# A decoder layer on one core: opening rewritten around the tokens, normalized tokens spread over the units that precede their use, stores from two queues

## The chip, the core and the metric

The kernel runs on one core of a Trainium2 chip. TensorE multiplies matrices (PE in the profile, its weight loads PEld), VectorE (DVE) and ScalarE (ACT) do elementwise work, and transfers between the main memory and the on-chip memory go through the core's 16 DMA engines; a transfer is started from the queue of SyncE (SP) or of ScalarE. The engines run side by side and wait for each other by semaphores, each working through its own list of instructions in order. The metric is the device time of one execution in microseconds; lower is better.

## The reference, cut to what matters

One decoder layer on 256 tokens of width 2048, in float32:

```
mod = silu(c) @ w_ada + b_ada                    # 2048 -> 6 x 2048: shift, scale, gate, twice
h   = rms_norm(x, norm1_g) * (1 + scale1) + shift1
lru_x, lru_gate, q, k, v, g_a, g_b = split(h @ w_in)
y_a = (rg_lru(conv4(lru_x)) * gelu(lru_gate)) @ w_lru_out
y_b = sliding_window_attention(q, k, v, sinks, bias) @ w_attn_out
x   = x + gate1 * ((sigmoid(g_a)*y_a + sigmoid(g_b)*y_b) @ w_out)
h2  = rms_norm(x, norm2_g) * (1 + scale2) + shift2
x   = x + gate2 * (relu(h2 @ w_ff1)**2 @ w_ff2)  # 2048 -> 8192 -> 2048
out = rms_norm(x, final_g)
```

## The kernel before, in words

*Layout.* Tokens lie along the free dimension: a tile is 128 channels by 256 tokens, and the width of 2048 is `KT` = 16 such tiles. A weight comes as units of 128 by 2048 float32 (1 MB), sixteen blocks of 128 by 128.

*Products.* A float32 product is made of three cheaper ones. Each operand is cut into a high part, rounded to the type `fp32r`, and the rest: `w_split` makes `wh` on ScalarE (L162) and `wl` on VectorE (L164) in two halves of 1024 columns, and `split` does the same for an activation tile (L143, L144). `gemm` then issues, for every block, `wh`·high, `wh`·low and `wl`·high into one PSUM tile (L178 to L180); `gemm_wide` joins the first two into one matmul of 512 columns (L191 to L194). Raw weights have four buffers (`RAW_BUFS`), `wh` and `wl` three each (`WH_BUFS`). All loads go through SyncE's queue in its order, so a load whose buffer is not free holds those behind it.

*Conditioning.* `mod` needs a product of one row with 96 units of weights. It is done on VectorE: `scr` holds silu(c) in every partition, and `ada_unit` loads a unit and reduces it against `scr` (L262, 128 by 2048). Two such units give shift and scale of one tile of `h`. 96 of them are scattered over the kernel by a credit.

*Opening.* Two small loads (`vc` with all vectors, `idt` the identity), eight loads of tokens of 128 by 512 (`xtok`, L97), all from SyncE. The line `scr` is built in four quarters by a multiply on VectorE (L222), a matmul with ones (L224) and a copy (L225). Squares of the tokens are summed, four on VectorE (L234) and four on ScalarE (L237); `rstd_cols` makes the factor per token in six small steps; VectorE scales the eight token pieces (L243); 32 transposes (L249) and eight copies (L251) turn them into channel-major tiles `xs`. Then two conditioning units give `a1` (L276), ScalarE applies shift and scale (L278), and `split` gives `h[j]`.

*Early passes.* So that TensorE need not wait for all sixteen `h`, the input projection first runs over `h[0:2]` for 56 output tiles (seven units), then `h[2:6]`, then `h[6:10]`, adding into `res` (L331 to L335); the rest of it comes in the main list of units.

*Main list.* Loads and splits are written two units ahead (`LOOK`); after a unit's `run`, side work is taken from a list by credit. The first nine units of the first feed-forward product (`run_first`, L687 to L689) start before the second normalization is known: they use un-normalized tiles `z` and multiply by the row factor in the eviction (L691 to L695). Units from the tenth on (`ZN_FROM` = 9) use normalized tiles `zn`, made by `make_zn` (L646, L647 and `split`), which come from the side list, all sixteen put there at the last output unit.

*End.* x is transposed back (L786), scaled by the last row factor, alternately on VectorE (L803) and ScalarE (L801), and written by eight stores from SyncE's queue (L804).

*Order.* A planner places the instructions on each engine, by its own model of durations and by the order in which they are written; it may put a later one first. `keep_in_program_order` pins an instruction behind the one that was written just before it on the same engine. Before, the pins that matter here are on reductions 0 and 4 only.

## Time and profile before

| what | value |
|---|---|
| three runs | 1597.89 us median (1596.14 to 1598.55) |
| the profiled execution | 1596.44 us, of which the span is 1594.7 us |
| TensorE / VectorE / ScalarE busy | 97% / 77% / 56% of the span |
| moved by DMA | 387.90 MB, 243 GB/s on average |

The span runs from the first to the last recorded instruction of one execution; the 1.7 us beside it lie outside it. "Busy" of TensorE is modelled from its pipelined matmuls. In a row of instructions the engine and the line of the kernel come first, then what is written and read with shapes, a count, and in brackets the idle time ahead and what ended it. A releaser is the one that came last.

### The profile page before, as it was taken

To read this page: it belongs to the slowest core of one execution; us is meant where nothing else is said; L and a number is where in the kernel's file an instruction comes from. 1 tells how busy PE (TensorE), PEld (TensorE's weight loads), DVE (VectorE), ACT (ScalarE), POOL (GpSimd) and SP (SyncE) were. 2 spreads that over 40 slices of the span, in tenths; PEclk is the share of its full clock that TensorE was granted. 3 is DMA by queue.
4 is the path that set the end of the run, shared out by engine and by line. 5 is a ranking of instruction groups with operands and counts; after the bars stand their busy time and mean duration, and the time that the engine had idled before them with its cause. 6 is when DMAs were issued, how large, how long until landed. Compare 5 with 4: busy or idle time off the path is not lost.

```text
span 1594.7 us, 24929 instructions
## 1 busy us (share of the span) xinstructions
PE 1552.5 (97%) x9804; PEld 1388.1 (87%) x9804; DVE 1220.7 (77%) x1947; ACT 888.5 (56%) x1508; POOL 0.2 (0%) x4
## 2 busy tenths in 40 slices
PE   4999999999999999999999999999999999999997
PEld 3999998899988888888888988888888888888886
DVE  6798998898989879788898867865565556655664
ACT  5733447687786564445456764356534664356554
POOL 0000000000000000000000000000000000000000
PEclk7999999999999999999999999999999999999999
DMA  8898985657768768778885667875555555555552
GB/s 315 330 341 318 340 287 196 214 180 243 277 234 301 264 230 304 284 290 294 320 314 207 221 243 271 320 266 185 185 186 187 189 192 194 189 185 185 185 187 78
DMA packets 61702, 387.90 MB, mean 243 GB/s; under 512 B 6576, under 2 KB 11024, under 8 KB 19216
## 3 DMA queue, kind: packets, MB, share of 16 engines
q1 hardware_dynamic: 57168, 381.95, 65.7%
q10 hardware_dynamic: 4416, 4.35, 1.0%
q8 instruction: 77, 1.26, 0.3%
q14 instruction: 41, 0.34, 0.1%
HBM read 384.13 MB, written 2.15 MB: 242 GB/s over the span
## 4 chain that ended last, share of the span: by engine, by line
PE 89%; DVE 5%; ACT 2%; issue 2%; DMA 1%; SPq 0%; ACTq 0%; DVEq 0%
PE pg L192 45%; PE pg L191 21%; PE pg L180 5%; PE pg L178 5%; PE pg L179 5%; DVE wl L164 2%; PE pg L207 2%; PE pg L194 1%; PE pg L689 1%; PE pg L687 1%; PE pg L688 1%; PE pa L491 1%; PE pa L498 1%; DVE ra L262 1%; ACT wh L162 1%
## 5 line engine op out<-in xcount | busy, mean ns | idle before, releaser
L192 PE MATMUL pg<-k,wh 128*128 128x512 f32 x3120 | 1080.4, 395 | 0.3 <-DVE k L144 0.3
L164 DVE TENSOR_TENSOR wl<-rw,wh 128x1024 fp32r<-128x1024 f32 (+2 forms) x534 | 628.3, 1178 | 281.8 <-ACT wh L162 275.2
L162 ACT ACTIVATE wh<-rw 128x1024 fp32r<-128x1024 f32 (+2 forms) x534 | 544.2, 1022 | 525.9 <-PE pg L192 365.3
L191 PE MATMUL pg<-k,wl 128*128 128x256 f32 x2925 | 819.9, 280 | 0.1
L192 PEld LDWEIGHTS pg<-k,wh 128*128 128x128 f32 x3120 | 573.6, 188 | 121.3 <-PE pg L192 0.6
L191 PEld LDWEIGHTS pg<-k,wl 128*128 128x128 f32 x2925 | 552.2, 189 | 9.5 <-DVE wl L164 0.4
L178 PE MATMUL pg<-k,wh 128*128 128x256 f32 x832 | 237.4, 287 | 10.4 <-ACT k L143 8.9
L180 PE MATMUL pg<-k,wl 128*128 128x256 f32 x832 | 233.9, 284 | 3.7 <-DVE wl L164 3.6
L179 PE MATMUL pg<-k,wh 128*128 128x256 f32 x832 | 235.0, 283 | 0.2 <-DVE k L144 0.2
L262 DVE CUSTOM_DVE_ANT_0 ra<-ra,scr,vc 128x2048 f32<-128x2048 f32 x96 | 225.1, 2346 | 9.7 <-DMA ra<-in_wada_dram 9.6
L178 PEld LDWEIGHTS pg<-k,wh 128*128 128x128 f32 x832 | 157.4, 190 | 12.9 <-ACT k L143 9.4
L180 PEld LDWEIGHTS pg<-k,wl 128*128 128x128 f32 x832 | 157.2, 190 | 6.0 <-DVE wl L164 4.7
L179 PEld LDWEIGHTS pg<-k,wh 128*128 128x128 f32 x832 | 157.9, 190 | 1.2 <-DVE k L144 0.5
L712 DVE SCALAR_TENSOR_TENSOR k<-pg,mod,k 128x256 f32<-128x256 f32 x128 | 61.9, 483 | 31.8 <-PE pg L192 29.5
L701 ACT ACTIVATE t<-t 128x256 f32<-128x256 f32 x55 | 22.9, 417 | 70.5 <-DVE t L199 70.5
L194 PE MATMUL pg<-k,wl 128*128 128x256 f32 x195 | 55.2, 283 | 2.1 <-DVE wl L164 2.1
L199 DVE TENSOR_TENSOR t<-pg,t 128x256 f32<-128x256 f32 x131 | 54.7, 418 | 0.0
L198 ACT ACTIVATE t<-pg 128x256 f32<-128x256 f32 x131 | 47.8, 365 | 1.7 <-PE pg L192 1.7
L194 PEld LDWEIGHTS pg<-k,wl 128*128 128x128 f32 x195 | 36.6, 188 | 10.7 <-DVE wl L164 2.8
L687 PE MATMUL pg<-z,wh 128*128 128x258 f32 x144 | 41.6, 289 | 2.0 <-ACT wh L162 2.0
L689 PE MATMUL pg<-z,wl 128*128 128x258 f32 x144 | 41.5, 289 | 0.9 <-DVE wl L164 0.9
L688 PE MATMUL pg<-z,wh 128*128 128x256 f32 x144 | 41.7, 290 | 0.0
(158 smaller groups left out, 959.1 us busy)
## 6 DMA issues: line engine op xcount, KB each, us to landing
rw<-in_w_f_dram SPq DMA_DIRECT2D x204, 1024.0 KB, 4.9
ra<-in_wada_dram SPq DMA_DIRECT2D x96, 1024.0 KB, 6.5
rw<-in_w_p_dram SPq DMA_DIRECT2D x31, 1024.0 KB, 6.7
rw<-in_w_r_dram SPq DMA_DIRECT2D x20, 768.0 KB, 4.9
rw<-in_w_r_dram SPq DMA_DIRECT2D x16, 640.0 KB, 4.0
bt<-ud ACTq DMA_DIRECT2D x8, 512.0 KB, 4.2
xt<-in_xt_dram SPq DMA_DIRECT2D x8, 256.0 KB, 6.5
lw<-in_lruw_dram SPq DMA_DIRECT2D x4, 512.0 KB, 5.8
```

The source lines that it names most:

```text
L162: se.activation(wh[:, :c], raw[:, o:o + c], AF.Copy)
L164: ve.tensor_tensor(out=wl[:, :c], in0=raw[:, o:o + c], in1=wh[:, :c].bitcast(F32), op=ALU.subtract)
L178: te.matmul(ps, lhsT=wh[:, w], rhs=hl[:, 0], start=k == 0, stop=False)
L179: te.matmul(ps, lhsT=wh[:, w], rhs=hl[:, 1], start=False, stop=False)
L180: te.matmul(ps, lhsT=wl[:, w], rhs=hl[:, 0], start=False, stop=k == n - 1)
L191: te.matmul(ps[:, 0], lhsT=wl[:, w], rhs=hl[:, 0], start=False, stop=False)
L192: te.matmul(ps, lhsT=wh[:, w], rhs=hl, start=k == 0, stop=k == n - 1)
L194: te.matmul(ps[:, 0], lhsT=wl[:, w], rhs=hl[:, 0], start=False, stop=False)
L262: r = ve.tensor_tensor_reduce(out=raw, in0=raw, in1=scr, scale=1.0, scalar=vc[:, V_BADA + c:V_BADA + c + 1], op0=ALU.mult, op1=ALU.add, ac ...
L687: te.matmul(ps, lhsT=wh[:, e], rhs=z[k][:, 0:258], start=k == 0, stop=False)
L688: te.matmul(ps[:, 0:256], lhsT=wh[:, e], rhs=z[k][:, 258:514], start=False, stop=False)
L712: ve.scalar_tensor_tensor(out=x1[f], in0=ps[:, i], scalar=mod[:, 5 * KT + f:5 * KT + f + 1], in1=x1[f], op0=ALU.mult, op1=ALU.add)
```

## The change

- *Loads.* `vc` and `idt` are started from ScalarE's queue. The tokens come as four loads of 128 by 1024 from SyncE, into buffers of `wh` and `wl` that no weights use yet (two of three each). The first four conditioning units (`ada_dma`) and the first weight unit (`first_raw`) are issued from fixed places.
- *Line.* `line_quarter` transposes a broadcast column of `sc` sixteen times in place of multiply and matmul with ones.
- *Squares.* Five on VectorE and three on ScalarE, interleaved with the line's copies in a written order.
- *Turning.* Per quarter (`turn_in`), VectorE scales one half of the tokens and ScalarE the other.
- *Order.* Nearly all VectorE and ScalarE work of the opening is pinned (`pin`): turn quarters 0 and 1, reductions 0 and 1, split the first half of the first weights, `h[0]`, reduction 2, the second half, reduction 3, turn quarter 2, `h[1]`, turn quarter 3. Reductions 4 to 11 are pinned too; reduction 4 was before.
- *Normalized tokens.* `make_zn` is no longer on the side list. Unit f of `run_first` makes tiles 2f and 2f+1 after its own eviction, and their first step is pinned.
- *Stores.* Odd pieces are stored from ScalarE's queue, even ones from SyncE's.

`split` loses an argument that nothing used.

```diff
...
 ADA_LAST, QUIET_OUT, QUIET_FF1 = 0.3, 2, 3
 LOOK, CREDIT, Z_FROM, ADA_RATE, ADA_FIRST = 2, 2.3, 12, 0.45, 0.85
 
-ZN_FROM, ZN_COST = 9, 1.0
+ZN_FROM = 9
 
 PASSES = [(0, 2, 56), (2, 6, 56), (6, 10, 40)]
 NATIVE = {(2, u) for u in range(0, 56, 16)}
...
         return pa.tile(list(shape), F32, tag="pa", name=nm("pa"))
 
 
+    pin = tc.keep_in_program_order
     vc = cp.tile([P, NV], F32, name="vc")
-    nc.sync.dma_start(out=vc, in_=vec)
+    pin(se.dma_start(out=vc, in_=vec))
     idt = cp.tile([P, P], F32, name="idt")
-    nc.sync.dma_start(out=idt, in_=ident)
+    pin(se.dma_start(out=idt, in_=ident))
+
     xtok = {}
-    for b in range(2):
-        for q in range(4):
-            xtok[b, q] = kp.tile([P, 512], F32, tag="k2", name=nm("xt"))
-            nc.sync.dma_start(out=xtok[b, q], in_=xt[b, :, q * 512:(q + 1) * 512])
+    for i in range(2):
+        for b, tag in ((0, "wh"), (1, "wl")):
+            xh = wp.tile([P, WCH], F32R, tag=tag, name=nm(tag), bufs=WH_BUFS).bitcast(F32)
+            pin(nc.sync.dma_start(out=xh, in_=xt[b, :, i * WCH:(i + 1) * WCH]))
+            for q in range(2):
+                xtok[b, 2 * i + q] = xh[:, q * 512:(q + 1) * 512]
     ones = cp.tile([P, P], F32, name="ones")
     ve.memset(ones, 1.0)
     eps = cp.tile([P, 1], F32, name="eps")
     ve.memset(eps, EPS)
 
...
-    def w_split(raw, n):
+    def w_split(raw, n, pin=lambda i: i, o0=0):
         parts = []
-        for o in range(0, n, WCH):
-            c = min(WCH, n - o)
+        for o in range(o0, o0 + n, WCH):
+            c = min(WCH, o0 + n - o)
             wh = wp.tile([P, WCH], F32R, tag="wh", name=nm("wh"), bufs=WH_BUFS)
-            se.activation(wh[:, :c], raw[:, o:o + c], AF.Copy)
+            pin(se.activation(wh[:, :c], raw[:, o:o + c], AF.Copy))
             wl = wp.tile([P, WCH], F32R, tag="wl", name=nm("wl"), bufs=WH_BUFS)
-            ve.tensor_tensor(out=wl[:, :c], in0=raw[:, o:o + c], in1=wh[:, :c].bitcast(F32), op=ALU.subtract)
+            pin(ve.tensor_tensor(out=wl[:, :c], in0=raw[:, o:o + c], in1=wh[:, :c].bitcast(F32), op=ALU.subtract))
             parts.append((wh, wl))
         return parts
 
...
 
 
     sc = cp.tile([P, KT], F32, name="sc")
-    tc.keep_in_program_order(se.activation(sc, vc[:, V_C:V_C + KT], AF.Sigmoid))
-    ve.tensor_tensor(out=sc, in0=sc, in1=vc[:, V_C:V_C + KT], op=ALU.mult)
-
-    tc.keep_in_program_order(se.activation(tmp([P, 1]), ones[:, 0:1], AF.Sqrt))
+    pin(se.activation(sc, vc[:, V_C:V_C + KT], AF.Sigmoid))
+    pin(ve.tensor_tensor(out=sc, in0=sc, in1=vc[:, V_C:V_C + KT], op=ALU.mult))
+
+    pin(se.activation(tmp([P, 1]), ones[:, 0:1], AF.Sqrt))
     scr = cp.tile([P, KT * P], F32, name="scr")
-    for q in range(4):
-        pc = bank([P, 512])
-        dg = tmp([P, 512])
-        ve.tensor_tensor(out=dg.rearrange("p (k f) -> p k f", k=4), in0=idt[:, None, :].broadcast_to((P, 4, P)),
-                         in1=sc[:, 4 * q:4 * q + 4, None].broadcast_to((P, 4, P)), op=ALU.mult)
-        te.matmul(pc, lhsT=ones, rhs=dg, start=True, stop=True)
-        se.activation(scr[:, q * 512:(q + 1) * 512], pc, AF.Copy)
-
-
     ssq = sp.tile([P, 2, 4], F32, tag="ssq", name="ssq", bufs=1)
     ss1 = sp.tile([P, 2], F32, tag="ss1", name="ss1", bufs=1)
-    for b in range(2):
-        for q in range(4):
-            xq = xtok[b, q]
-            if b == 0:
-                ve.tensor_tensor_reduce(out=tmp([P, 512]), in0=xq, in1=xq, scale=1.0, scalar=0.0, op0=ALU.mult,
-                                        op1=ALU.add, accum_out=ssq[:, b, q:q + 1])
-            else:
-                se.activation(tmp([P, 512]), xq, AF.Square, accum_out=ssq[:, b, q:q + 1])
-    ve.tensor_reduce(out=ss1, in_=ssq, axis=mybir.AxisListType.X, op=ALU.add)
-    rs1 = rstd_cols(ss1)
+    def line_quarter(q):
+        pc = bank([P, 512])
+        for i in range(4):
+
+            k = 4 * q + i
+            te.transpose(pc[:, i * P:(i + 1) * P], sc[:, k:k + 1].broadcast_to((P, P)), idt)
+        pin(se.activation(scr[:, q * 512:(q + 1) * 512], pc, AF.Copy))
+
+    def square_dve(b, q):
+        pin(ve.tensor_tensor_reduce(out=tmp([P, 512]), in0=xtok[b, q], in1=xtok[b, q], scale=1.0, scalar=0.0,
+                                    op0=ALU.mult, op1=ALU.add, accum_out=ssq[:, b, q:q + 1]))
+
+    def square_act(b, q):
+        pin(se.activation(tmp([P, 512]), xtok[b, q], AF.Square, accum_out=ssq[:, b, q:q + 1]))
+
+
+    line_quarter(0)
+    square_dve(0, 0)
+    square_dve(0, 1)
+    square_act(1, 0)
+    square_act(1, 1)
+    line_quarter(1)
+    line_quarter(2)
+    square_dve(0, 2)
+    square_dve(0, 3)
+    square_act(1, 2)
+    square_dve(1, 3)
+    line_quarter(3)
+    pin(ve.tensor_reduce(out=ss1, in_=ssq, axis=mybir.AxisListType.X, op=ALU.add))
+    rs1 = rstd_cols(ss1, pin)
     xs = []
-    for q in range(4):
-        for b in range(2):
-            ve.tensor_scalar(out=xtok[b, q], in0=xtok[b, q], scalar1=rs1[:, b:b + 1], scalar2=None, op0=ALU.mult)
+
+    def turn_in(q):
+
+        pin(ve.tensor_scalar(out=xtok[0, q], in0=xtok[0, q], scalar1=rs1[:, 0:1], scalar2=None, op0=ALU.mult))
+        pin(se.activation(xtok[1, q], xtok[1, q], AF.Copy, scale=rs1[:, 1:2]))
         for j in (2 * q, 2 * q + 1):
             px = bank([P, 512])
             for i in range(2):
...
                     e = (2 * (j % 2) + i) * P
                     te.transpose(px[:, i * T + b * P:i * T + (b + 1) * P], xtok[b, q][:, e:e + P], idt)
             xs.append(pair())
-            se.activation(xs[j].rearrange("p a b -> p (a b)"), px, AF.Copy)
+            pin(se.activation(xs[j].rearrange("p a b -> p (a b)"), px, AF.Copy))
+
 
     mod = cp.tile([P, 6 * KT], F32, name="mod")
     ada_next = [0]
-
-    def ada_unit():
+    same = lambda i: i
+
+    def ada_dma(pin=same):
+        raw = wp.tile([P, KT * P], F32, tag="raw", name=nm("ra"), bufs=RAW_BUFS)
+        pin(nc.sync.dma_start(out=raw, in_=wada[ada_next[0] + len(ada_raw)]))
+        ada_raw.append(raw)
+
+    ada_raw = []
+
+    def ada_unit(pin=same):
+        if not ada_raw:
+            ada_dma()
+        raw = ada_raw.pop(0)
         n = ada_next[0]
         ada_next[0] += 1
-        raw = wp.tile([P, KT * P], F32, tag="raw", name=nm("ra"), bufs=RAW_BUFS)
-        nc.sync.dma_start(out=raw, in_=wada[n])
         c = ADA_ORDER[n]
-        r = ve.tensor_tensor_reduce(out=raw, in0=raw, in1=scr, scale=1.0, scalar=vc[:, V_BADA + c:V_BADA + c + 1],
-                                    op0=ALU.mult, op1=ALU.add, accum_out=mod[:, c:c + 1])
-
-        if n in (0, 4):
-            tc.keep_in_program_order(r)
+
+        if 2 * PASSES[0][1] <= n < 2 * PASSES[0][1] + 8:
+            pin = tc.keep_in_program_order
+        pin(ve.tensor_tensor_reduce(out=raw, in0=raw, in1=scr, scale=1.0, scalar=vc[:, V_BADA + c:V_BADA + c + 1],
+                                    op0=ALU.mult, op1=ALU.add, accum_out=mod[:, c:c + 1]))
         return n
 
     h = [None] * KT
     a1 = cp.tile([P, KT], F32, name="a1")
+
     def ada_norm1():
         n = ada_unit()
         if n % 2 == 1:
-            j = n // 2
-            xj = xs[j // 2][:, j % 2]
-            ve.scalar_tensor_tensor(out=a1[:, j:j + 1], in0=mod[:, KT + j:KT + j + 1], scalar=1.0,
-                                    in1=vc[:, V_G1 + j:V_G1 + j + 1], op0=ALU.add, op1=ALU.mult)
-            se.activation(xj, xj, AF.Identity, scale=a1[:, j:j + 1], bias=mod[:, j:j + 1])
-            h[j] = split(xj)
-
-    for _ in range(2 * PASSES[0][1] - 2):
-        ada_norm1()
+            norm1_tile(n // 2)
+
+    def norm1_tile(j, pin=same):
+        xj = xs[j // 2][:, j % 2]
+        pin(ve.scalar_tensor_tensor(out=a1[:, j:j + 1], in0=mod[:, KT + j:KT + j + 1], scalar=1.0,
+                                    in1=vc[:, V_G1 + j:V_G1 + j + 1], op0=ALU.add, op1=ALU.mult))
+        pin(se.activation(xj, xj, AF.Identity, scale=a1[:, j:j + 1], bias=mod[:, j:j + 1]))
+        h[j] = split(xj, pin)
+
+
+    ada_dma(pin)
+    ada_dma(pin)
+    first_raw = w_dma(w_p[0], 2048, pin)
+    ada_dma(pin)
+    turn_in(0)
+    turn_in(1)
+    ada_unit(pin)
+    n1 = ada_unit(pin)
+    first_w = w_split(first_raw[0], WCH, pin)
+    norm1_tile(n1 // 2, pin)
+    ada_dma(pin)
+    ada_unit(pin)
+    first_w += w_split(first_raw[0], WCH, pin, WCH)
+    n1 = ada_unit(pin)
+    turn_in(2)
+    norm1_tile(n1 // 2, pin)
+    turn_in(3)
 
 
     relt = cp.tile([32, NH], F32, name="relt")
...
         per = KT // kw
         for u in range(0, n, per):
             nf = min(per, n - u)
-            raw = w_dma(w_p[n_pass, :, 0:nf * kw * P], nf * kw * P)
+            raw = w_dma(w_p[n_pass, :, 0:nf * kw * P], nf * kw * P) if n_pass else first_raw
             n_pass += 1
             while h[k1 - 1] is None:
                 ada_norm1()
...
                 for i in range(nf):
                     add_part(gemm_native(raw[0], i * kw, k0, k1), u + i)
             else:
-                wts = w_split(*raw)
+                wts = first_w if n_pass == 1 else w_split(*raw)
                 for i in range(nf):
                     add_part(gemm(wts, i * kw, h[k0:k1]), u + i)
             ada_due += ADA_FIRST
...
     def make_zn(f):
 
         t = tmp([P, T])
-        ve.tensor_tensor(out=t, in0=x1[f], in1=stat[2], op=ALU.mult)
+        pin(ve.tensor_tensor(out=t, in0=x1[f], in1=stat[2], op=ALU.mult))
         se.activation(t, t, AF.Identity, scale=a2[:, f:f + 1], bias=mod[:, 3 * KT + f:3 * KT + f + 1])
         zn[f] = split(t)
 
...
             if f == 15:
                 flush()
                 stat[2] = rstd_of(stat[2])
-                for i in range(16):
-                    later(ZN_COST, make_zn, i)
         add_unit(run)
 
 
...
             se.activation(t[:, 0], t[:, 0], AF.Relu, bias=sh)
             se.activation(t[:, 1], t[:, 0], AF.Square)
             ff[c, f] = split(t[:, 1])
+            for k in (2 * f, 2 * f + 1):
+                if k < KT:
+                    make_zn(k)
 
         def run(w):
             t = tmp()
...
             se.activation(o[:, :ca], pt[:, :ca], AF.Copy, scale=rs3[:, b:b + 1])
         if ca < 512:
             ve.tensor_scalar(out=o[:, ca:], in0=pt[:, ca:], scalar1=rs3[:, b:b + 1], scalar2=None, op0=ALU.mult)
-        nc.sync.dma_start(out=out[b, :, q * 512:(q + 1) * 512], in_=o)
+        (se if n % 2 else nc.sync).dma_start(out=out[b, :, q * 512:(q + 1) * 512], in_=o)
 
 
 # ---- launch: one core; the host only lays the arrays out ----
```

29 lines of the change are left out of this document (12 added, 17 removed).

## The prediction

> **What bounds the kernel now.** I read the page first: the share of each engine and the forty slices.
>
> ```profile
> span 1594.7 us, 24929 instructions
> PE 1552.5 (97%) x9804; PEld 1388.1 (87%) x9804; DVE 1220.7 (77%) x1947; ACT 888.5 (56%) x1508; POOL 0.2 (0%) x4
> PE   4999999999999999999999999999999999999997
> PEclk7999999999999999999999999999999999999999
> ```
>
> TensorE is busy for 1552.5 of 1594.7 us, so 42.2 us of idle time plus the time lost to a low clock is all that a reordering can win. Slice 1 (busy 4, clock 7) and the last one (7) hold most of it. The waits of TensorE say where it stands still:
>
> ```profile
> PE pg L178 <- ACT k L143: 8.9, 2, 4.8
> PE pa L249 <- issue: 6.6, 1, 6.6
> ...
> PE pg L687 <- ACT wh L162: 2.0, 1, 2.0
> PE pg L689 <- DVE wl L164: 0.9, 1, 0.9
> ```
>
> The first two lie in the opening (tokens in, first weights). The last two are one hole where the first feed-forward product begins. These are the two places that the change touches, besides the stores behind the last matmul. Everything else stands, and I leave it at zero.
>
> **Opening, as it is.** Windows of 10 us (after the stretch: busy us and count of PE, PEld, DVE, ACT, POOL, then granted clock, DMA share, GB/s), then the rows of the timeline that form its chain:
>
> ```profile
> 0.00:10.00 10.00, 5.69 (x8) 2.21 (x8) 5.47 (x15) 3.58 (x5) 0.20 (x4) 1.00 0.65 200
> 10.00:20.00 10.00, 3.43 (x17) 3.19 (x17) 4.81 (x15) 5.90 (x15) 0.00 (x0) 0.78 1.02 426
> 80.00:100.00 20.00, 18.53 (x140) 17.53 (x139) 18.60 (x29) 6.82 (x8) 0.00 (x0) 1.00 0.96 358
> ...
> 0.73 0.38 SPq L90 DMA_DIRECT2D vc<-in_vec_dram  x1
> 3.11 0.21 ACT L214 ACTIVATE sc<-vc 128x16 f32<-128x16 f32 x1 [1.10 <-DMA vc<-in_vec_dram]
> 1.64 3.88 SPq L97 DMA_DIRECT2D xt<-in_xt_dram  x8
> 10.63 0.63 ACT L237 ACTIVATE t<-xt 128x512 f32<-128x512 f32 x1 [3.61 <-DMA xt<-in_xt_dram]
> 13.99 0.63 ACT L237 ACTIVATE t<-xt 128x512 f32<-128x512 f32 x1
> 14.74 0.16 DVE L238 TENSOR_REDUCE ss<-ssq 128x2 f32<-128x8 f32 x1 [4.89 <-ACT t L237]
> 16.16 3.26 DVE L243 TENSOR_SCALAR xt<-xt,st 128x512 f32<-128x512 f32 x8
> 19.34 2.35 DVE L262 CUSTOM_DVE_ANT_0 ra<-ra,scr,vc 128x2048 f32<-128x2048 f32 x1
> 20.43 0.60 ACT L251 ACTIVATE k<-pa 128x512 f32<-128x512 f32 x1 [0.26 <-PE pa L249]
> 32.06 2.35 DVE L262 CUSTOM_DVE_ANT_0 ra<-ra,scr,vc 128x2048 f32<-128x2048 f32 x1
> 34.52 0.60 ACT L278 ACTIVATE k<-k,mod,a 128x256 f32<-128x256 f32 x1 [7.25 <-DVE a L276]
> 35.15 0.42 ACT L143 ACTIVATE k<-k 128x256 fp32r<-128x256 f32 x1
> 35.62 0.79 PE L178 MATMUL pg<-k,wh 128*128 128x256 f32 x2 [4.75 <-ACT k L143]
> ...
> 83.05 2.35 DVE L164 TENSOR_TENSOR wl<-rw,wh 128x1024 fp32r<-128x1024 f32 x2
> ```
>
> To be seen: the row statistics wait for the tokens (10.63) and then for ScalarE's four squares in a row, so the normalization starts only at 16.16. VectorE then carries everything: eight scalings, five conditioning reductions of 2.3 us (the fifth, at 32.06, is not needed yet) and two splits. TensorE runs without a break only from 35.62, when `h[1]` exists.
>
> **Opening, part by part.** X is the moment when the last tokens have landed. Before, the fifth of eight quarters landed at 10.63 and the last square, which waited for nothing, began at 13.99; the quarters are issued 0.48 apart (3.88/8), so the eighth landed some 1.45 after the fifth: X = 12. After, the token loads begin where `vc` began (0.73 for 1.64: 0.9 us) and are four of 512 KB with rows twice as long. What longer rows bring no row shows. One end: nothing, X = 11.1. The other: the 2.1 MB of tokens (256 by 2048 float32) at the 426 GB/s of the second window, 4.9 us, plus 0.73 and the 2.4 us that `vc` took from issue to use (0.73 to 3.11), X = 8.0. I take 10.0, nearer the slow end, since the first window moved only 200 GB/s at a DMA share of 0.65. `vc` and `idt` now go out from ScalarE ahead of its table load, two issues of some 0.4 us, hidden behind the token wait of 3.61 us on the ACT row; without that cover they would cost 0.8. The line copies lose VectorE's four multiplies and use sixteen transposes; both lie in the token wait.
>
> From X on I walk through the pinned order, using 2.3 for a reduction, 1.15 for a split (two in a row take 2.35), 0.41 for a scaling (3.26/8), 0.6 for an eviction (20.43). Last square 0.7 and reduce, then the 1.42 from reduce to normalization (14.74 to 16.16): statistics at X+2.4. VectorE: two scalings and two reductions, to X+7.8. ScalarE meanwhile: two scalings and four evictions behind their transposes, to X+8.2, then the first `wh` (about 1.0), so `wl` runs X+9.3 to X+10.5; `a1`, L278, L143: first matmul at X+11.7. VectorE goes on: 0.4 (low part), 2.3, 1.15, 2.3, 0.4 for the scaling of `turn_in(2)`: X+18.2. Only then its eight transposes (0.21 us each, as the matmuls below run at the lower clock: 1.7), the last eviction 0.6, and L278 with L143, 1.0: `h[1]` at X+21.5 = 31.5, against 35.6 before. That is 4.1 us earlier: 2.0 from X, 2.5 from the shorter statistics (2.4 for 4.2), less the rest. The fifth reduction has left the path, but `turn_in(2)` has entered it.
>
> Two things are given back. `turn_in(3)` is behind `h[1]`, so eight transposes that lay in idle time now run inside the matmul stream: 8 times 0.12 = 1.0 us (1.7 at the lower clock). And around 80 to 100 us the DMA share is 0.96 while TensorE already stands still for 1.5 us: what arrives 3 us sooner there meets weights that don't. I take 0.6, ends 0 and 2. The opening thus brings 4.1 - 1.0 - 0.6 = 2.5 us; its ends are 6.1 (X = 8.0, nothing given back) and -0.7 (X = 11.1, 1.7 and 2 given back).
>
> **Feed-forward start.** The windows in and behind the hole, TensorE's rows at its edge and in its wake, ScalarE's rows ahead of it, and the window of the whole stage:
>
> ```profile
> 875.00:880.00 5.00, 2.15 (x12) 1.73 (x11) 4.99 (x11) 5.00 (x11) 0.00 (x0) 0.91 0.30 123
> 880.00:885.00 5.00, 5.00 (x35) 5.00 (x33) 5.00 (x9) 3.74 (x8) 0.00 (x0) 0.75 0.67 220
> 885.00:890.00 5.00, 5.00 (x44) 5.00 (x43) 3.91 (x8) 4.51 (x9) 0.00 (x0) 1.00 0.95 383
> ...
> 874.93 0.28 PE L688 MATMUL pg<-z,wh 128*128 128x256 f32 x1
> 875.05 0.28 PE L689 MATMUL pg<-z,wl 128*128 128x258 f32 x1
> 880.05 0.42 PE L687 MATMUL pg<-z,wh 128*128 128x258 f32 x1
> 880.26 0.42 PE L688 MATMUL pg<-z,wh 128*128 128x256 f32 x1
> ...
> 868.79 1.09 ACT L647 ACTIVATE t<-t,mod,a 128x256 f32<-128x256 f32 x2 [0.49 <-DVE t L646]
> 876.23 1.99 ACT L162 ACTIVATE wh<-rw 128x1024 fp32r<-128x1024 f32 x2
> ...
> 856.40:915.90 59.50, 56.60 (x448) 55.76 (x447) 50.76 (x97) 44.58 (x81) 0.00 (x0) 0.97 0.60 215
> ```
>
> From 868.79 ScalarE makes normalized tokens in a burst, and the weights' `wh` come only at 876.23. TensorE waits for them (the two L687 and L689 rows above, 2.9 us), and comes back at a lower clock: matmuls 0.21 apart (880.05 to 880.26) that ran 0.12 apart ahead (874.93 to 875.05). In the first ten microseconds of these windows it runs 47 matmuls, where 88 fit by the third window: 41 times 0.114 (5.00/44), 4.7 us lost in all. The change ties two tiles to each unit's eviction: tiles 14 and 15 come behind unit 7, and unit 9 is the first to read them, one unit of 48 matmuls (48 times 0.12 = 5.8 us) later, which covers their chain of some 2 us. In the stage window VectorE is busy for 50.8 us and ScalarE for 44.6; without the hole it has 59.5 - 4.7 = 54.8. So it fits, tightly; a stalled eviction, with the pinned token multiply queued behind it and the next split behind that, could still make TensorE wait. I take 4.2; ends 0 (the hole only moves) and 4.7.
>
> **Stores.** The end of the two engines, the queue, and the transfers:
>
> ```profile
> 1585.88 2.42 ACT L801 ACTIVATE t<-pa,st 128x512 f32<-128x512 f32 x4
> 1586.59 4.48 SPq L804 DMA_DIRECT2D out_dram<-t  x8
> ...
> 1588.00:1590.00 2.00, 0.00 (x0) 0.00 (x0) 0.00 (x0) 0.30 (x1) 0.00 (x0) 0.77 1.04 375
> ```
>
> Eight issues take 4.5 us, but the 2.1 MB need 5.6 us at 375 GB/s, and the DMA share is full: the engines set the end. What two queues can win is the start: the first tile's ScalarE half is done by 1585.88, the queue begins at 1586.59, so 0.7, and one issue of 0.56, at best 1.3 together. Against that, ScalarE's four remaining evictions now alternate with four issues of its own: 1585.88 + 4 x (0.6 + 0.56) = 1590.5 for its last issue, near the 1591.1 at which the last one ends now, and a wait of 0.35 in each pair would put it 0.8 later (end: -0.8). I take 0.5.
>
> The Trainium skill, in "DMA: Bandwidth & Descriptors", section "Issuing engines are not separate DMA queues", says that transfers begun from several engines run on the same 16 DMA engines and that only the time of the issue is saved. The full share in these rows agrees, and by the rule alone this part would be worth about 0 and the sum 6.7.
>
> **The sum.** 2.5 + 4.2 + 0.5 = 7.2 us. The profiled execution took 1596.44 (its span 1594.7 and 1.7 around it), so 1589.2 by its own time; the median of the three runs, 1597.89, lies 1.45 higher: 1590.7.
>
> **The rivals.**
>
> 1. *The opening's gain is eaten by transfers.* The weights bound 80 to 100 us (share 0.96, TensorE idle 1.5 us there already), so an earlier start only waits longer. Against it: before 60 us the DMA engines were not full (0.65 in the first window). Left: 4.2 + 0.5, giving 1593.2.
> 2. *The hole of the feed-forward start moves but stays.* For it: VectorE at 50.8 of 54.8 us. Against it: tiles have a unit of slack. Left: 2.5 + 0.5, giving 1594.9.
> 3. *The pinned order stalls VectorE: slower.* Reductions 4 to 11 now hold their written place, so one whose weights land late holds the next unit's split behind it, and TensorE waits. The trace has such a wait already, in this very stage (first all 96 reductions with their idle time ahead, then the one):
>
> ```profile
> L262 DVE CUSTOM_DVE_ANT_0 ra<-ra,scr,vc 128x2048 f32<-128x2048 f32 x96 | 225.1, 2346 | 9.7 <-DMA ra<-in_wada_dram 9.6
> ...
> 78.42 2.35 DVE L262 CUSTOM_DVE_ANT_0 ra<-ra,scr,vc 128x2048 f32<-128x2048 f32 x1 [1.84 <-DMA ra<-in_wada_dram]
> ```
>
> Eight such waits, all passed on to TensorE, cost 14.7 us: 1597.89 - 7.2 + 14.7 = 1605.4. It outweighs the gains from 0.9 us per reduction. Against it: all 96 reductions together waited 9.6 us.
> 4. *It does not do what it says.* The planner still places what is not pinned, the transposes above all; if they fall behind first matmuls that wait, `h[1]` comes no earlier, and later wishes of the planner shift as well. Only the stores remain: 1597.4.
>
> **How the numbers follow.** Forecast 55%, rivals 18, 12, 6 and 9%. The prediction is 1590.7. What can be told from no change is 0.2%, or 3.2 us: 1594.7 to 1601.1. Faster: 52 of the forecast's 55, 15 of the 18, 5 of the 12, 72%; slower: rival 3 and a little of the fourth, 7%; the same: 21%. The forecast's own ends are 1597.89 - 12.1 = 1585.8 (6.1 + 4.7 + 1.3) and, with the opening at its bad end and the rest as taken, 1593.9. The range reaches on over rivals 1, 2 and 4, to 1597.5; outside stay rival 3 and the tails.
>
> **What would show it.** Tokens: last token square ready near 10 to 11, normalization at X+2.4. Opening: `h[1]` at 31.5 and the unbroken stretch of TensorE from there; if the split waits on the reduction's DMA in 40 to 80 us, rival 3; if TensorE's wait in 80 to 100 us grows from 1.5 to over 3 us, rival 1. Feed-forward start: the waits L687 and L689 gone and no window with a clock under 1.00. Stores: first issue near 1586 less the rest's gain, the DMA share full for 5 us as before. The prediction is wrong if the first matmuls move earlier and the last do not.

## The result, and the profile after

The changed kernel took 1589.09 us in the median of four runs, against 1597.7 for the kernel before beside it: 0.9944 of its time, 95% interval 0.9926 to 0.9963. A second comparison gave 1589.12 against 1598.3, 0.9938 (0.9924 to 0.9952). So it is faster, by 8.6 and 9.2 us; predicted were 1590.7 and a gain of 7.2. The profiled execution took 1585.86, the shortest of its four, so gains read from its profile come out larger than these.

The page of the changed kernel, then what its TensorE waited for (total, times, longest, us). Its conditioning reduction is now L287, the first feed-forward product L726 to L728, the early products L177 to L179.

```profile
span 1584.1 us, 24932 instructions
PE 1543.9 (97%) x9812; PEld 1383.8 (87%) x9812; DVE 1216.9 (77%) x1941; ACT 890.9 (56%) x1510; POOL 0.2 (0%) x4
...
L287 DVE CUSTOM_DVE_ANT_0 ra<-ra,scr,vc 128x2048 f32<-128x2048 f32 x96 | 225.1, 2346 | 14.4 <-DMA ra<-in_wada_dram 14.3
```

```profile
PE pa L225 <- DMA idt<-in_ident_dram: 7.0, 1, 7.0
PE pa L261 <- issue: 6.5, 2, 3.6
PE pg L177 <- ACT k L146: 5.7, 2, 4.1
PE pg L179 <- DVE wl L163: 3.6, 4, 1.7
```

The two waits of the first feed-forward product are gone. The three largest that are left lie in the opening, which the timeline shows (start, duration, what, idle time ahead and its releaser):

```profile
0.73 0.41 ACTq L91 DMA_DIRECT2D vc<-in_vec_dram  x1
5.41 0.22 ACT L213 ACTIVATE sc<-vc 128x16 f32<-128x16 f32 x1 [2.48 <-DMA vc<-in_vec_dram]
7.00 3.65 PE L225 MATMUL pa<-idt,sc 128*128 128x128 f32 x16 [7.00 <-DMA idt<-in_ident_dram]
8.21 0.69 DVE L229 CUSTOM_DVE_ANT_0 t<-wh 128x512 f32<-128x512 f32 x1 [1.16 <-DMA wh<-in_xt_dram]
9.45 0.69 DVE L229 CUSTOM_DVE_ANT_0 t<-wl 128x512 f32<-128x512 f32 x1
9.85 1.07 ACT L226 ACTIVATE scr<-pa 128x512 f32<-128x512 f32 x2
11.56 0.16 DVE L248 TENSOR_REDUCE ss<-ssq 128x2 f32<-128x8 f32 x1 [1.41 <-ACT t L233]
12.99 0.88 DVE L254 TENSOR_SCALAR wh<-wh,st 128x512 f32<-128x512 f32 x2
21.83 0.80 PE L177 MATMUL pg<-k,wh 128*128 128x256 f32 x2 [4.10 <-ACT k L146]
28.41 0.45 PE L261 MATMUL pa<-idt,wh 128*128 128x128 f32 x1 [3.62 <-issue]
31.98 1.22 PE L177 MATMUL pg<-k,wh 128*128 128x256 f32 x4 [1.62 <-ACT k L146]
33.64 0.41 PE L261 MATMUL pa<-idt,wh 128*128 128x128 f32 x1
35.01 0.27 PE L261 MATMUL pa<-idt,wl 128*128 128x128 f32 x1
```

VectorE's last token square starts at 9.45 without a wait, so all tokens that it reads are there by then. The statistics are late all the same (11.56): ScalarE's line copies stand among its squares, and they wait for `idt`, which came only at 7.00. From the normalization (12.99) on, the walk holds: `h[0]` at 21.83, the third quarter's transposes at 28.41, `h[1]` at 31.98, where before it was 35.62. The fourth quarter's eight transposes then run inside the stream (33.64 to about 35.1).

The windows of the feed-forward start and of the stretch of rival 1 (columns as in the prediction):

```profile
875.00:880.00 5.00, 5.00 (x44) 5.00 (x44) 4.12 (x8) 4.09 (x9) 0.00 (x0) 1.00 0.52 185
880.00:885.00 5.00, 5.00 (x44) 5.00 (x43) 4.81 (x8) 4.12 (x8) 0.00 (x0) 1.00 0.46 151
885.00:890.00 5.00, 5.00 (x44) 5.00 (x43) 4.92 (x12) 4.11 (x9) 0.00 (x0) 1.00 0.82 301
...
80.00:100.00 20.00, 18.58 (x149) 17.74 (x148) 18.61 (x28) 5.77 (x8) 0.00 (x0) 1.00 0.96 360
```

TensorE runs 44 matmuls in each 5 us at full clock; the hole and its slow wake are gone. From 80 to 100 us it stands still for 1.42 us, as before (1.47). The end:

```profile
1575.30 2.47 SPq L846 DMA_DIRECT2D out_dram<-t  x4
1575.67 0.96 ACTq L846 DMA_DIRECT2D out_dram<-t  x2
1577.67 1.41 ACTq L846 DMA_DIRECT2D out_dram<-t  x2
```

```profile
1578.00:1580.00 2.00, 0.00 (x0) 0.00 (x0) 0.00 (x0) 0.22 (x1) 0.00 (x0) 0.50 1.04 356
1580.00:1582.00 2.00, 0.00 (x0) 0.00 (x0) 0.00 (x0) 0.00 (x0) 0.00 (x0) 0.50 0.92 341
```

The last issue is over at 1579.1; the DMA engines stay full until the 2.1 MB are out.

**Where each kernel gained.** I compare each profile with that of before by the moment at which the same instruction ran. The *lead* is the time before minus the time in that run (us); the columns are what a stretch added to it. The marks: the last scaled addition of the early passes (191.9 before), the last tile of the residual sum (862.0), the last matmul of L687 in the nine units that start the first feed-forward product (914.4; L726 in the changed kernel), the last eviction of the second product (1582.4), the end of the span. The times are rounded to 0.1, and so an entry can be off by 0.1.

```
                   opening  to    feed-fwd  to 2nd   tail   lead in
                   (190 us) 862   start     product         all
changed kernel       2.6    1.6     5.1      1.6     -0.3    10.6
the same, again      1.3    1.6     5.1      1.6     -0.4     9.2
zn_only              0.7    1.3     5.0      0.4     -0.2     7.2
open_only            1.6    1.0     0.2      0.6     -0.4     3.0
stores_only          0.5   -2.2     1.1      0.0      0.2    -0.4
no_burst             0.2   -2.8     4.5      0.3      0.0     2.2
vc_sp                1.0   -2.9     5.1      1.6     -0.2     4.6
unpin                0.1    0.4     5.1      1.6     -0.3     6.9
zn_eight             1.5    2.3   -15.4      2.3     -0.3    -9.6
turn_early           2.0    0.5     5.2      1.9     -0.2     9.4
the same, again      3.5   -0.2     5.2      2.0     -0.3    10.2
```

One profile isn't enough for the opening: with the opening of before, the runs lead by 0 (before itself), 0.7, 0.5 and 0.2, mean 0.35; with the changed opening by 2.6, 1.3, 1.6 and 1.5 (`zn_eight`), mean 1.75. So traces put the opening at 1.4, give or take 0.7. The feed-forward start repeats to 0.2 among the seven traces here with the new token order, two tiles per unit; with the order of before it scatters from 0 to 1.1. The two kernels with five raw buffers (experiment 7) are not in the table.

### The profile page after: what moved, and what is told of

Read it like the earlier page. It is cut to its first block, busy times and chain, and to the rows that moved or that the text cites. A ratio compares the mean times of both kernels' runs of the same rounds, so it can differ in the third digit from the quotient of the medians.

```text
span 1584.1 us, 24932 instructions
## 1 busy us (share of the span) xinstructions
PE 1543.9 (97%) x9812; PEld 1383.8 (87%) x9812; DVE 1216.9 (77%) x1941; ACT 890.9 (56%) x1510; POOL 0.2 (0%) x4
## 4 chain that ended last, share of the span: by engine, by line
PE 86%; DVE 5%; DMA 4%; issue 3%; ACT 2%; ACTq 0%; DVEq 0%
PE pg L191 41%; PE pg L190 20%; PE pg L179 5%; PE pg L177 5%; PE pg L178 5%; DMA ra<-in_wada_dram 3%; DVE wl L163 2%; PE pg L206 2%; PE pg L193 1%; PE pg L727 1%; PE pg L728 1%; PE pg L726 1%; DVE ra L287 1%; PE pa L532 1%; PE pa L539 1%
## 5 line engine op out<-in xcount | busy, mean ns | idle before, releaser
L161 ACT ACTIVATE wh<-rw 128x1024 fp32r<-128x1024 f32 (+2 forms) x534 | 545.0, 1022 | 509.0 <-PE pg L191 353.3
L177 PE MATMUL pg<-k,wh 128*128 128x256 f32 x832 | 237.6, 287 | 7.4 <-ACT k L146 5.7
L179 PE MATMUL pg<-k,wl 128*128 128x256 f32 x832 | 233.6, 284 | 3.6 <-DVE wl L163 3.6
L287 DVE CUSTOM_DVE_ANT_0 ra<-ra,scr,vc 128x2048 f32<-128x2048 f32 x96 | 225.1, 2346 | 14.4 <-DMA ra<-in_wada_dram 14.3
L177 PEld LDWEIGHTS pg<-k,wh 128*128 128x128 f32 x832 | 157.5, 190 | 10.0 <-ACT k L146 6.5
L179 PEld LDWEIGHTS pg<-k,wl 128*128 128x128 f32 x832 | 156.5, 189 | 6.2 <-DVE wl L163 4.9
L726 PE MATMUL pg<-z,wh 128*128 128x258 f32 x144 | 40.7, 282 | 0.0
L728 PE MATMUL pg<-z,wl 128*128 128x258 f32 x144 | 40.6, 282 | 0.0
```

Source lines behind the costliest of these rows:

```text
L161: pin(se.activation(wh[:, :c], raw[:, o:o + c], AF.Copy))
L177: te.matmul(ps, lhsT=wh[:, w], rhs=hl[:, 0], start=k == 0, stop=False)
L179: te.matmul(ps, lhsT=wl[:, w], rhs=hl[:, 0], start=False, stop=k == n - 1)
L287: pin(ve.tensor_tensor_reduce(out=raw, in0=raw, in1=scr, scale=1.0, scalar=vc[:, V_BADA + c:V_BADA + c + 1], op0=ALU.mult, op1=ALU.add, ac ...
L726: te.matmul(ps, lhsT=wh[:, e], rhs=z[k][:, 0:258], start=k == 0, stop=False)
```

## The experiments

**1. Each part alone.** The changed kernel taken apart into its three parts, each put into the kernel before. First the normalized tokens:

```diff
-ZN_FROM, ZN_COST = 9, 1.0
+ZN_FROM = 9
...
-                for i in range(16):
-                    later(ZN_COST, make_zn, i)
...
             ff[c, f] = split(t[:, 1])
+            for k in (2 * f, 2 * f + 1):
+                if k < KT:
+                    make_zn(k)
```

> Only the normalized tokens of the change (two per unit behind its eviction, first step pinned), on the kernel before. My theory: the hole behind the first feed-forward units and its slow wake were 4.7 us and go as a whole; between the first matmul of that stage and the last one the stretch is 57.9 us before and 53 here, the waits of the first feed-forward product on `wh` and `wl` (2.9 us) are gone, and the time is 4 to 5 us under that of before. Rival (the hole only moves): another wait of TensorE of over 2 us in the stage, time within 1.5 us of before.

Measured: 1593.69 us, ratio 0.9967 (0.9955 to 0.998), so 5.3 us in time (3.2 to 7.2) and 5.0 in the trace, with no wait of TensorE from 845 to 935 us.

Then the opening alone: the changed kernel with the old side list for the normalized tokens, their first step not pinned, and the old stores.

```diff
-            for k in (2 * f, 2 * f + 1):
-                if k < KT:
-                    make_zn(k)
...
+                for i in range(16):
+                    later(ZN_COST, make_zn, i)
...
-        (se if n % 2 else nc.sync).dma_start(out=out[b, :,
+        nc.sync.dma_start(out=out[b, :,
```

> Only the opening of the change (loads, line, pinned order), with the old place of the normalized tokens and one store queue. My theory: the second h tile at 31.9 us as in the changed kernel (before: 35.6), of which 2.5 us are left from the second pass on, and 2.5 us in the time; the hole of 4.7 us in the feed-forward start stays as before. Rival (the rest of the change's gain, 3 to 4 us more than my sum at the end of the changed kernel's trace, comes from the opening too): 5 us or more.

Measured: 1595.05 us, ratio 0.9987 (0.9977 to 0.9997): 2.1 us (0.5 to 3.7). The hole of the feed-forward start stands as before (0.2 gained there).

Then the stores alone:

```diff
-        nc.sync.dma_start(out=out[b, :,
+        (se if n % 2 else nc.sync).dma_start(out=out[b, :,
```

> Only the stores from two queues, on the kernel before. Theory from the changed kernel's trace: the first store is issued some 0.4 us sooner after the last transpose, and the transfers end no sooner (from the last transpose's start to the end of the span 8.8 us before, 9.1 in the changed kernel): between -0.5 and +0.5 us, nothing that can be told in the time. Rival (two queues win the start, as I predicted): 0.5 to 1.3 us less from the last transpose to the end.

Measured: 1597.91 us, ratio 0.9999 (0.9988 to 1.001). From the start of the last transpose to the end of the span, kernels with SyncE's queue alone take 8.7 to 9.1 us and those with two queues 8.5 to 9.1. The stores are worth nothing that shows. The Trainium skill, "DMA: Bandwidth & Descriptors", section "Issuing engines are not separate DMA queues", had said so: the same 16 engines carry it, whoever issues. These runs agree.

The three gains add to 5.3 + 2.1 + 0.2 = 7.6 us, with some 3 us of uncertainty; together they measured 8.6 and 9.2.

**2. Was it the burst that made the hole?** The kernel before, with its side list stopped at the last output unit only; the normalized tokens then come from the list a few at a time:

```diff
+        if n == n_ff1 - 1:
+            credit = 0.0
         while credit > 0 and side:
```

> The kernel before with one edit: the side list's credit is set to zero at the last output unit, so that the normalized tokens still come from the side list, but at 2.3 per unit and with no burst at the start. If the burst on ScalarE made the hole, it goes here too (waits of the first feed-forward product under 1 us, stage 53 to 54 us). If the place behind the eviction or the pin is what helps, the hole stays (over 2 us).

Measured: 1594.56 us in its one run, beside a median of 1598.19. The windows of this kernel where the hole was:

```profile
870.00:880.00 10.00, 10.00 (x84) 9.95 (x83) 8.89 (x17) 8.27 (x19) 0.00 (x0) 1.00 0.32 107
880.00:890.00 10.00, 10.00 (x85) 10.00 (x85) 10.00 (x22) 8.42 (x17) 0.00 (x0) 1.00 0.82 315
```

TensorE runs through, at 84 and 85 matmuls in 10 us where the changed kernel has 88. The stretch gains 4.5 of the 5.0. So the burst was the cause, by one trace with a clear sign, and the place behind the eviction, pinned or not, is worth at most the last 0.5.

**3. How tight is the place behind the eviction?** Eight tiles behind units 0 and 1 each, in place of two behind each of eight:

```diff
-            for k in (2 * f, 2 * f + 1):
+            for k in range(8 * f, 8 * f + 8):
```

> The changed kernel with the sixteen normalized tokens made eight behind the eviction of unit 0 and eight behind that of unit 1, in place of two behind each of eight units. If a burst ahead of the weights' `wh` makes the hole, it comes back here: waits of the first feed-forward product on `wh` and `wl` of 2 to 4 us and a window with a clock under 1.00. If only the side list's place made it, none comes (under 1 us).

Measured: 1606.08 us in one run, 17.0 above the changed kernel's median. Its TensorE waits, and two of its windows:

```profile
PE pg L726 <- DVE t L732: 16.2, 2, 10.9
```

```profile
880.00:900.00 20.00, 10.32 (x73) 9.94 (x71) 13.39 (x25) 12.84 (x23) 0.00 (x0) 0.87 0.47 170
900.00:920.00 20.00, 13.46 (x92) 13.49 (x93) 10.81 (x24) 12.53 (x26) 0.00 (x0) 0.70 0.16 52
```

A burst is worse here than in the side list: 16.2 us against the 2.9 of before. I expected TensorE to wait for weights, but the releaser is VectorE's multiply of an eviction (L732), the step that reads the products out of PSUM. In VectorE's written order it comes behind the steps of the eight tiles of the unit before, which go to ScalarE and back one after the other. The small sum ahead of it (L730) ran at 877.24, the multiply only at 887.73; until then the PSUM tile did not come free. VectorE is not full meanwhile (13.39 of 20 us). It is the prediction's warning come true, a stalled eviction, and it shows what two per unit avoid.

**4. The small loads on the other queue.** The changed kernel with `vc` and `idt` issued from SyncE ahead of the tokens, as before:

```diff
-    pin(se.dma_start(out=vc, in_=vec))
+    pin(nc.sync.dma_start(out=vc, in_=vec))
...
-    pin(se.dma_start(out=idt, in_=ident))
+    pin(nc.sync.dma_start(out=idt, in_=ident))
```

> The changed kernel with the vectors and the identity loaded from SyncE ahead of the tokens, as before. Theory: from ScalarE's queue they shared the transfers with the tokens and came late (first use of the identity at 7.0 us), which made ScalarE's line copies and squares end the statistics at 11.6 us. Here the identity is used by 4.5 us, the tokens come 0.9 us later, and the statistics are reduced at 11.0 to 11.3. Rival (the tokens are the bound): reduced at 12.2 or later.

Measured: 1591.85 us in one run; lead at 190 us 1.0, where the same opening has 1.3 to 2.6. Its timeline:

```profile
3.15 0.22 ACT L213 ACTIVATE sc<-vc 128x16 f32<-128x16 f32 x1 [1.14 <-DMA vc<-in_vec_dram]
10.21 0.69 DVE L229 CUSTOM_DVE_ANT_0 t<-wh 128x512 f32<-128x512 f32 x1 [2.48 <-DMA wh<-in_xt_dram]
12.25 0.16 DVE L248 TENSOR_REDUCE ss<-ssq 128x2 f32<-128x8 f32 x1
```

`vc` is used at 3.15, not 5.41, but the third token load at 10.21, not 8.21. In the changed kernel the two queues share the DMA engines, and what the tokens win the vectors lose: 2.0 for 2.3. The statistics then come 0.7 later (12.25 for 11.56), because the tokens are needed last. My expectation, that the statistics would come sooner since the line copies no longer stood in the way, was wrong; the rival of the expectation, that the tokens are the bound, held (12.25 for "12.2 or later"). The move helps: in the nine other profiles with the changed loads the normalization starts at 12.99 to 13.39 us, here at 13.67. What that is worth in time, 0.3 to 1.6 us by the leads, rests on this one trace.

**5. The pinned reductions.** The changed kernel without the pins of reductions 4 to 11 (rival 3):

```diff
-        if 2 * PASSES[0][1] <= n < 2 * PASSES[0][1] + 8:
-            pin = tc.keep_in_program_order
```

> The changed kernel without the pins on reductions 4 to 11. VectorE waited 14.3 us for conditioning weights in the changed kernel, 9.6 before. If the pins cost (rival 3 of the prediction): that wait falls under 11 and the second pass begins 1 us sooner or more (first L333 at 84 us or less, 85.1 in the changed kernel). If they help or do nothing, that start lies within 0.7 us of the changed kernel's or later.

Measured: 1589.54 us in one run. The waits of VectorE for reductions' weights from 30 us on, the first row without these pins (30 to 90 us, its line is L285), the second of the changed kernel (30 to 100 us):

```profile
DVE ra L285 <- DMA ra<-in_wada_dram: 2.8, 2, 2.4
```

```profile
DVE ra L287 <- DMA ra<-in_wada_dram: 1.5, 1, 1.5
```

So they don't stall VectorE: in all it waits 12.6 us for such weights without the pins and 14.4 with them, but that costs nothing. The mark that I had named, the first scaled addition, can't tell (86.5 us without them, 85.1 and 86.4 in the two profiles of the changed kernel). The lead can: from the last eviction of the first pass (75.8 us before) to 190 us the nine profiles with these pins add some 0.2 each to theirs, and this one loses 1.0, from 1.1 to 0.1. So in the trace the pins help, by some 1.2 us. Its one time is no worse than the changed kernel's median, so the sign rests on that trace.

**6. Turning the last quarters early.** A version that might beat both: scalings of quarters 2 and 3 are put into VectorE's and ScalarE's gaps, so that all transposes are done ahead of `h[1]`:

```diff
+    scale_dve(2)
+    scale_dve(3)
     first_w = w_split(first_raw[0], WCH, pin)
...
     first_w += w_split(first_raw[0], WCH, pin, WCH)
+    scale_act(2)
+    scale_act(3)
+    turn(2)
+    turn(3)
     n1 = ada_unit(pin)
-    turn_in(2)
     norm1_tile(n1 // 2, pin)
-    turn_in(3)
```

> The changed kernel with quarters 2 and 3 of the tokens scaled on VectorE ahead of the first weight split (where it waited 1 us for `wh`), and on ScalarE and turned between the second `wh` and reduction 3 (where ScalarE waited 6 us). Theory: the turn of quarter 2 held the second h tile by 2.9 us and the turn of quarter 3 cost the matmul stream 1.5 us, so the second h tile comes at 29.0 (31.9 in the changed kernel), the first eviction 4 us sooner, and the time is 3 to 4 us under the changed kernel's (0.9920 of before or less). Rival (transfers bound 80 to 100 us): the lead is lost there, TensorE's waits from 45 to 110 us grow from 1.4 to over 4 us, and the time is that of the changed kernel (0.9945).

Measured: 1586.91 us, ratio to before 0.9922 (0.9902 to 0.9942). `h[1]` comes at 30.07 (expected 29.0) and the first eviction 5.5 us ahead of before, against 1.1 for the changed kernel; but at 190 us the lead is 2.0. A part went to the slow clock, which lasted through the window

```profile
30.00:36.00 6.00, 5.93 (x27) 5.93 (x28) 5.27 (x6) 3.88 (x9) 0.00 (x0) 0.50 0.99 406
```

and the rest between 52 and 72 us, where SyncE's issues had stopped (38.2 to 44.4 us) and the DMA share fell to 0.55. I blamed the four raw buffers.

**7. Five raw buffers, and both kernels again beside them.** The room for a fifth buffer is taken from the `k2` tiles:

```diff
-RAW_BUFS, WH_BUFS, WCH = 4, 3, 1024
+RAW_BUFS, WH_BUFS, WCH = 5, 3, 1024
...
-    kp = ctx.enter_context(tc.tile_pool(name="kp", bufs=49))
+    kp = ctx.enter_context(tc.tile_pool(name="kp", bufs=48))
```

> The kernel with quarters 2 and 3 turned early, now with five raw weight buffers in place of four (and 48 in place of 49 k2 tiles to make the room). Theory, four raw buffers lost what the early turn had gained: the gap in SyncE's issues between 38.2 and 44.4 us closes, ScalarE's waits for raw weights before 90 us (5.1 us with four) go under 1.5, VectorE's and TensorE's windows of 52 to 72 us fill (35 to 36 matmuls in each 4 us, against 31, 25 and 34), and the lead over before at the first output of the second kind of pass (85 us) is 4 us or more in place of 1.9. Rival, the transfers' own rate: the DMA share goes to 0.95 or more in each window from 36 to 76 us, the raw waits stay at 3 us or more, and the lead at 85 us stays within 1.2 and 2.6. Time by the theory 2 us below the same kernel with four buffers, by the rival the same within 1.

> The kernel with the early turn again, beside the changed kernel on the same chip, to tell whether it is the faster of the two. By its trace (a lead of 1.9 us after the opening against 2.6) it should be 0 to 1 us slower than the changed kernel; by its first times (1586.9 against 1589.1) 2 us faster.

> The changed kernel with five raw weight buffers in place of four and 48 k2 tiles. It turned the last quarters where the change does, so h[1] comes at 31.9 us. Theory, the four buffers cost it too: its lead of 2.6 us at 85 us was 3.6 at h[1], and rises to 3.3 or more. Rival, by then the transfers alone set it: 2.6 within 0.4. In both, if the 49th k2 tile was needed later, a wait for a k2 tile that the changed kernel does not have shows between 220 and 1570 us.

> The changed kernel again. Its profiled runs have a lead of 2.6 us at 85 us, 4.2 at 860, 9.3 at 905 and 10.9 at 1575; of these the changed parts explain 7.3, and the rest came in stretches in which the two programs are the same. If that rest is drift between executions, it comes out otherwise here: the lead at 85 us 2.6 and the gain across the feed-forward start 5.0, each within 0.4, and the rest anything between -3 and 4.

Measured, beside 1598.3: `turn_raw5` 1595.59 (0.9981, 0.997 to 0.9991), `after_raw5` 1597.5 (0.9994, 0.9985 to 1.0004), `turn_again` 1587.17 (0.9932, 0.992 to 0.9945), `after_again` 1589.12 (0.9938, 0.9924 to 0.9952). The two windows that should have filled, in `turn_raw5` and then in `turn_again`:

```profile
52.00:56.00 4.00, 3.87 (x31) 3.46 (x30) 2.49 (x3) 3.61 (x9) 0.00 (x0) 1.00 0.88 358
64.00:68.00 4.00, 2.87 (x22) 2.46 (x22) 2.09 (x4) 3.54 (x7) 0.00 (x0) 1.00 1.01 422
```

```profile
52.00:56.00 4.00, 3.92 (x31) 3.50 (x30) 2.73 (x4) 3.57 (x8) 0.00 (x0) 1.00 0.82 336
64.00:68.00 4.00, 2.89 (x22) 2.48 (x21) 2.25 (x3) 3.36 (x7) 0.00 (x0) 1.00 0.97 397
```

They did not: 31 and 22 matmuls of some 36 in both. And in `turn_again` ScalarE waited for no raw weights at all from 30 to 75 us, with four buffers, at a DMA share of 0.82 in the first of these windows. The gap in SyncE's issues did not close either (37.8 to 43.4 us in `turn_raw5`), and `after_raw5` leads by 1.5 at 190 us, no more than with four buffers. So neither the raw buffers nor the transfers' rate is it, and both of my theories fall. The timeline of `turn_again` in the second hole names another chain:

```profile
61.22 2.35 DVE L294 CUSTOM_DVE_ANT_0 ra<-ra,scr,vc 128x2048 f32<-128x2048 f32 x1
63.61 0.16 DVE L308 SCALAR_TENSOR_TENSOR a<-mod,vc 128x1 f32<-128x1 f32 x1
64.03 0.59 ACT L310 ACTIVATE k<-k,mod,a 128x256 f32<-128x256 f32 x1
64.78 0.41 ACT L146 ACTIVATE k<-k 128x256 fp32r<-128x256 f32 x1
65.09 1.05 ACT L161 ACTIVATE wh<-rw 128x1024 fp32r<-128x1024 f32 x1
66.19 0.39 PE L177 MATMUL pg<-k,wh 128*128 128x256 f32 x1 [1.06 <-ACT wh L161]
```

TensorE waits for a weight's high part (L161); that stands on ScalarE behind the shift and scale of the next tile of `h` (L310), which needs VectorE's reduction (L294, 2.35 us, over at 63.6). The first hole, at 53 us, has the same order of rows. An earlier `h[1]` so runs into the pace at which conditioning makes the next `h`: from 40 to 72 us this kernel's TensorE runs 252 matmuls and the changed kernel's 274, and 22 at 0.117 (32.00/274) are 2.6 us. That is read from the trace; no run changed that chain alone. The same trace has a rival to it: ahead of these holes VectorE stood still for 2.76 us, until 40.20, for a `wl` buffer that TensorE had yet to free, with its next reductions queued behind. No run changed the three buffers of `WH_BUFS`.

The raw-buffer kernels lose some 8 us on their twins, in the traces mostly behind 862 us (7.0 of 8.4, and 7.5 of 10.2 for `after_raw5`); whether the `k2` tile given up or the fifth buffer does it was not separated.

Does the early turn beat the changed kernel? Its medians are lower by 2.2 and 2.0 us, the opening's lead by its two traces higher by 0.8 (2.75 and 1.95), but the intervals overlap both times. Over nine runs of each the means are 1587.2 and 1588.7, and their spreads (1584.9 to 1590.1, 1585.9 to 1592.1) leave the 1.5 us uncertain by about as much. It is probably a little faster, and not shown.

## Why the prediction was right, step by step

- *Feed-forward start, 4.2 (0 to 4.7).* Right in place and mechanism, undersized: 5.0 to 5.2 in seven traces, above the upper end, which counted only the ten microseconds of the hole and its wake. That the burst made it is shown by experiment 2. Rival 2 (the hole moves) fell, but experiment 3 shows how it could have come true: with eight tiles behind an eviction TensorE waits 16 us.
- *Opening, 2.5 (-0.7 to 6.1).* Oversized: 1.4 by traces, 2.1 (0.5 to 3.7) by time. The walk itself met its marks: `h[1]` at 31.98 for 31.5, 3.6 us earlier for 4.1. Within it two steps failed and nearly cancelled: X was taken as 10.0 and is below 9.5, and the issues of `vc` and `idt` from ScalarE were costed at nothing, hidden behind the token wait. The issue is hidden; the data is not, it came 2.3 us later, and the copies that wait for it pushed the normalization to 12.99 where X + 2.4 would be 11.9. On balance the move still pays (experiment 4). In the prediction's account of its 4.1 us one figure is off: from 4.2 to 2.4 the statistics gain 1.8, not 2.5, so the rest adds 0.3; the sum does not depend on it.
- *Transposes in the stream, -1.0.* Measured about 1.5 (33.64 to 35.01 and the last one's 0.12), between the figures for the two clocks, 1.0 and 1.7.
- *Transfers, -0.6 between 80 and 100 us.* That stretch lost nothing (1.42 idle for 1.47), and the changed kernel's lead of 2.4 us at the last eviction of the first pass is still 2.6 at 190. So rival 1 fell. Its counter-argument was weak all the same: it cites the DMA share of 0.65 of the first window, but the next window shown, 10 to 20 us, has 1.02. Where `h[1]` comes earlier still (experiments 6 and 7) much of the gain is taken back, at 52 to 68 us; by the trace VectorE's reductions and the splits behind them on ScalarE do that, not the transfers' rate; no run tested that chain alone.
- *Stores, 0.5 (-0.8 to 1.3).* Nothing. The first issue does come earlier, 0.3 us after the start of the last transpose in place of 0.6, but the DMA engines set the end. The value of 0 by the Trainium skill's rule was the better choice.
- *Rival 3, pinned reductions.* Fell, and by the one trace without the pins its sign is wrong: reductions waited 14.4 us for weights in all (9.7 before), yet without the pins the opening loses 1.0 us where it gains 0.2 with them (from 76 to 190 us).
- *Rival 4.* Fell: the early stretch and the stores ran as written.
- *The sum, 7.2.* By traces the named parts give 1.4 + 5.1 - 0.3 = 6.2; measured are 8.6 and 9.2. The near hit in the total is thus in part luck: it has help from elsewhere. Some 1.6 us come behind the changed stretches, from 905 us to the last product, and that is no scatter: in the table it is 1.6 to 2.3 in each kernel that has both a new opening and tokens made behind evictions, and at most 0.6 where one of them is missing. The two kernels with five raw buffers have both as well and lose 3.2 and 4.3 there, so it is not these two parts alone that set it. Between 905 and 1580 us TensorE waits for nothing, before or after. Its windows in a part of that stretch, before and then after:

```profile
1000.00:1300.00 300.00, 300.00 (x1715) 262.35 (x1714) 189.75 (x230) 150.74 (x222) 0.00 (x0) 1.00 0.60 217
```

```profile
1000.00:1300.00 300.00, 300.00 (x1724) 262.89 (x1723) 187.07 (x229) 153.62 (x230) 0.00 (x0) 1.00 0.60 214
```

Nine matmuls more in 300 us of a fully busy TensorE at the same granted clock: a slightly closer pace (9 times 0.174 is 1.6 us). What sets it stays open. Between 190 and 862 us the lead moves by -2.9 to +2.3 with no pattern by part, which I take for differences between executions.

## What to carry to other kernels

Work put on a list in one burst ahead of a stage can make a hole by its burst alone; stopping it for one unit brought nine tenths of what the rewrite brought there (4.5 of 5.0 us). But small work tied to an eviction is only safe in small portions: with eight tiles the eviction itself waited and the hole grew more than fivefold. When an opening is moved up, follow each queue behind the new start: a small load sent beside a large one from another queue is not free, and the next chain in line (here, by the trace, conditioning, shift and scale, split) can take back much of a gain.

## What the runs showed of the hardware that I had not expected

- *Two queues share.* The load of `vc`, issued at 0.73 either way, was used at 3.15 ahead of the token loads in SyncE's queue and at 5.41 beside them from ScalarE's; the third token load at 10.21 and 8.21.
- *The slow clock lasts differently.* In `turn_early` matmuls ran 0.21 us apart from 30.07 to 36.03, 6.0 us with next to no gap; in the changed kernel, after its last pause, only from 31.98 to 34.7, so the fast clock came while its transposes were running. In `turn_again`, the same kernel as `turn_early`, the granted clock was 1.00 at first (29.6 to 31.4 us), then 0.50 in the middle of unbroken work (31.4 to 34.8), then 1.00 again; before, the slow pace lasted from 35.62 to 39.2. The Trainium skill, "TensorE: Matmul & The Clock Gate", part on the HAM clock gate, gives a warm-up of about 3.4 us of sustained work, watched in a free-running window. The 2.7 us here and the 6.0 there straddle that figure, and by these two a change in the opening can win or lose some 1.6 us (an estimate: half of the 3.3 us between them, since the pace halves).
- *Same code, other phase.* Two profiles of the changed kernel had `h[1]` at 31.98 and 32.77, and leads at 190 us of 2.6 and 1.3. An opening worth 1 to 2 us can't be sized from one profile.
